# A linear-attention kernel: the level queries of GLA in one product, the level differences in one subtraction

## The chip, the core and the metric

The kernel runs on one core of a Trainium2 chip. The core has a matrix engine (TensorE, PE in the profile; its weight loads are PEld), a vector engine (VectorE, DVE), an activation engine (ScalarE, ACT), a general engine (GpSimd, POOL) and an engine that issues DMAs (SyncE, SP). Each runs its own queue in order and waits on semaphores for the others. The metric is the time of one execution on the device, in microseconds (us).

## The reference, cut to what matters

One step of a two-layer decoder for 512 prompt tokens and 64 sample tokens (8 sequences of 8). Each layer projects the normed input, feeds four recurrent mixers (HGRN2, GLA, RWKV-7, retention), gates and merges them, and ends with a SwiGLU feed-forward. HGRN2 and GLA are gated linear attention: a decay of its own for each key channel and token.

```python
    def step(S, inp):
        qb, kb, vb, gb = inp
        b = jnp.cumsum(gb, axis=2)
        diff = b[:, :, :, None, :] - b[:, :, None, :, :]
        decay = jnp.exp(jnp.where(causal > 0, diff, 0.0)) * causal
        scores = jnp.sum(qb[:, :, :, None, :] * kb[:, :, None, :, :] * decay, axis=-1)
        o = (jnp.einsum('bhts,bhsv->bhtv', scores, vb)
             + jnp.einsum('bhtk,bhkv->bhtv', qb * jnp.exp(b), S))
...
    o_gla, n_gla = gated_linear_attention_chunked(
        _heads(gla_q * GLA_DK ** -0.5, GLA_H), _heads(gla_k, GLA_H),
        _heads(gla_v, GLA_H), _heads(log_a, GLA_H), s_gla)
```

HGRN2 has four heads with 64 key channels each, GLA four with 32; both have 64 value channels a head.

## The kernel before

Channels lie on the 128 partitions and tokens along the free axis. HGRN2 has two tiles of channels with two heads each (nt = 2), GLA one tile with four heads of 32 partitions (nt = 1). `gla_core` (L967) serves both. It takes the running sums B of the log decays and goes over five chunks: four of 128 prompt tokens and one of the 64 sample tokens.

Within a chunk the scores are built by levels: m = 64, 32, 16, 8, 4, 2, 1 for a prompt chunk, m = 4, 2, 1 for the sample chunk. At level m the chunk falls into blocks of 2m tokens; queries of a block's later half (u = 1) meet keys of its earlier half (u = 0), with B at the first token of the later half as the common reference. So the exponents are ref - B for the earlier half and B - ref for the later one, and neither grows. `gla_level` (L1089) does one level:

- L1101 and L1102: two subtractions on VectorE, one per half, into the tile le
- L1103: one exponential on ScalarE over the whole of le, in place
- L1104: the keys times le into lk, on VectorE for HGRN2 and on GpSimd for GLA
- L1111: the queries of the later halves times le into a zero-padded tile that holds every head apart, qt for HGRN2 (two products of 64 partitions) and qg for GLA (four of 32 partitions, and half of the chunk's tokens as columns)

L1018 multiplies the two on TensorE into lvp, with all four heads side by side along the free axis, and `gla_pred` (L1122) copies the valid places of it into the score tile sc on VectorE (L1126). The loop is staggered: the operands of the next level are made ahead of the product of the present one, and the predicated copy of a level comes after that.

The padded tiles come from three-deep rings (`padded`, L1114) that GpSimd zeroes once (L412 to L414); only the diagonal blocks of heads are written afterwards.

The mixers are generators. `mix` (L1612) advances them between the steps of the projection's units, by the paces of PACE (L43): HGRN2 beside the RWKV and GLA projections, GLA beside later projections and gates, RWKV over nearly the whole. The matrix products of the units have weights that are split into two halves of 16 bits (L228 on ScalarE, L229 on VectorE), and their matmuls are L241 to L243. The recurrent RWKV state is updated at L867 on VectorE, after TensorE's product L865, and TensorE's products L815 and L849 wait for it; GpSimd's copy L795 and its other small steps serve the same recurrence. The instructions are put in order on each engine by a planner that works from its own estimates of their costs; the order on an engine is thus not always that of the code.

Of the kernel before, what the change touches and what calls it, by code (L numbers as in the profile page):

```python
# [10 lines left out]
F32 = mybir.dt.float32  # L11
F16 = mybir.dt.float16
I32 = mybir.dt.int32
AF = mybir.ActivationFunctionType
ALU = mybir.AluOpType
PSUM = bass.MemoryType.PSUM
ADD, SUB, MUL, MAX, MIN = ALU.add, ALU.subtract, ALU.mult, ALU.max, ALU.min
# [157 lines left out]
class Net:  # L175
# [159 lines left out]
    def setup(self):  # L335

        nc, t, cp = self.nc, self.io, self.cp
        rows = self.wp.tile([128, GW], F32, tag="raw", name="prow")[:, :128]
        for n, k in PARAMS:
            b = PBASE[n][0]  # L340
# [14 lines left out]
        for i, a in enumerate(self.x0):  # L355
            k, hs = 2 * (i % 4), slice(HW * (i // 4), HW * (i // 4) + HW)
# [16 lines left out]
        for n in ("rw_w0", "rw_a0"):  # L373
            b, k = PBASE[n]
            nc.vector.tensor_scalar(self.pc[:, b:b + 2 * k], self.pc[:, b:b + 2 * k], 0.5, None, op0=MUL)
        b = PBASE["rw_kk"][0]
        nc.vector.tensor_scalar(self.pc[:, b:b + 4], self.pc[:, b:b + 4], 2.0 ** 15, None, op0=MUL)
        b = PBASE["rw_ka"][0]
# [3 lines left out]
        b = PBASE["hg_lb_logits"][0]  # L382
# [15 lines left out]

        self.qt = [cp.tile([128, 4, 64], F32, name=f"qt{i}") for i in range(3)]
        self.qg = [cp.tile([128, 4, 64], F32, name=f"qg{i}") for i in range(3)]  # L400
        self.sc = [cp.tile([128, 4, 128], F32, name=f"sc{i}") for i in range(2)]
        self.scs = cp.tile([64, 4, 64], F32, name="scs")
        self.vz = [cp.tile([128, 2, 256], F32, name=f"vz{i}") for i in range(2)]
# [5 lines left out]
        self.xb = cp.tile([128, 2, 64], F32, name="rw_xb")  # L409
        self.qb = [cp.tile([128, 2, 128], F32, name=f"rt_qb{i}") for i in range(2)]  # L410
        self.nkv = 0
        for a in [*self.kvb, *self.abk, self.ab, self.ub, *self.bb, self.xb, *self.qb, *self.qt, *self.qg,  # L412
                  *self.sc, self.scs, *self.vz]:
            nc.gpsimd.memset(a, 0.0)  # L414
        self.nq = self.nqg = self.nsc = self.nvz = 0
# [551 lines left out]
    def gla_core(self, l, q, k, v, lg, nt, load, result):  # L967
# [3 lines left out]
        nc = self.nc  # L971
        hpt = 4 // nt
        dk = 128 // hpt
        B = lg
# [21 lines left out]
        for c in range(5):  # L996
            samp = c == 4
            n = 64 if samp else 128
            ts = slice(128 * c, 128 * c + n)
# [4 lines left out]
                sc = self.sc[self.nsc % 2]  # L1004
                self.nsc += 1
            lv = [(li, m) for li, m in enumerate(LEVELS) if 2 * m <= (8 if samp else 128)]
            ops = [self.gla_level(q, k, B, nt, ts, n, m) for li, m in lv[:1]]
            prev = None
            for i, (li, m) in enumerate(lv):
                if i + 1 < len(lv):  # L1010
                    ops.append(self.gla_level(q, k, B, nt, ts, n, lv[i + 1][1]))
                if prev is not None:
                    self.gla_pred(*prev)
                yield
                kt, qt = ops[i]
                ps = self.psum("g", [128, 4, 64], f"lvp{nt}")
                for j in range(nt):
                    nc.tensor.matmul(ps[:n, hpt * j:hpt * j + hpt, :n // 2], kt[:, j],  # L1018
                                     qt[:, hpt * j:hpt * j + hpt, :n // 2], start=True, stop=True)
                prev = sc, ps, li, m, n  # L1020
# [4 lines left out]
            w = 8 if samp else 128  # L1025
            nc.scalar.activation(QH, B[:, :, ts], AF.Exp)
            bb = B[:, :, ts].rearrange("p j (c s) -> p j c s", s=w)
# [4 lines left out]
            if samp:  # L1032
                qz = self.padded(nt)
                for h in range(hpt):
                    r = slice(dk * h, dk * h + dk)
# [9 lines left out]
            ops = self.psum("g", [128, 2, 128], "gop")  # L1045
# [40 lines left out]
        result += [O, S]  # L1086
        yield

    def gla_level(self, q, k, B, nt, ts, n, m):  # L1089

        nc = self.nc
        hpt = 4 // nt
        dk = 128 // hpt
        nb = n // (2 * m)
        E = self.t("gt", [128, nt, n], f"le{nt}")
        kt = self.t("gt", [128, nt, n], f"lk{nt}")

        eng = nc.vector
        bb, ee = (a.rearrange("p j (b u i) -> p j b u i", u=2, i=m) for a in (B[:, :, ts], E))
        ref = bb[:, :, :, 1, 0:1].to_broadcast([128, nt, nb, m])  # L1100
        eng.tensor_tensor(ee[:, :, :, 0], ref, bb[:, :, :, 0], op=SUB)  # L1101
        eng.tensor_tensor(ee[:, :, :, 1], bb[:, :, :, 1], ref, op=SUB)  # L1102
        nc.scalar.activation(E, E, AF.Exp)  # L1103
        (nc.vector if nt == 2 else nc.gpsimd).tensor_tensor(kt, k[:, :, ts], E, op=MUL)  # L1104
        qt = self.padded(nt)
        for h in range(hpt):
            r = slice(dk * h, dk * h + dk)
            qq = q[r, :, ts].rearrange("p j (b u i) -> p j b u i", u=2, i=m)[:, :, :, 1]
            ee = E[r].rearrange("p j (b u i) -> p j b u i", u=2, i=m)[:, :, :, 1]
            qo = qt[r, h::hpt, :n // 2].rearrange("p j (b i) -> p j b i", i=m)  # L1110
            nc.vector.tensor_tensor(qo, qq, ee, op=MUL)  # L1111
        return kt, qt

    def padded(self, nt):  # L1114
# [497 lines left out]
    def mix(self, l, prepared):  # L1612
# [3 lines left out]
        for half in range(2):  # L1616
            for i in range(3):
                for _ in range(2):
                    next(units[i])
                if half == 0 and i == 0:  # L1620
                    if l:
                        self.norm_half("attn_norm_w", l, 1)
                    else:
                        self.first_norm(1)
                        setup = self.setup()
                        next(setup)
                if l == 0 and half == 1 and i == 0:
                    run(setup)
# [314 lines left out]
```

## Time and profile before

| what | us |
|---|---|
| median of 3 runs (lowest, highest) | 2242.47 (2237.26, 2242.92) |
| the profiled execution | 2235.82 |
| its span, first to last instruction | 2234.1 |
| PE busy | 2047.3 (92%) |
| PEld busy | 1616.7 (72%) |
| DVE busy | 1677.4 (75%) |
| ACT busy | 1070.6 (48%) |
| POOL busy | 652.0 (29%) |

Busy time is the union of an engine's records. Matmuls are pipelined and their ends are modelled, so a busy TensorE is not yet one at its peak. The chain of work that ended last is followed back from the last instruction, at each step to what released it or to the instruction ahead of it on its engine. A group's row gives its busy time, the mean duration of one instruction, and the idle time of the engine just before, with who ended it. Layer 0 takes the first half of the span, layer 1 the second.

### The profile page before, as it was taken

How to read it: one execution, taken by the hardware profiler on the slowest of the kernel's cores; microseconds unless marked ns; L12 is line 12 of the kernel's file. 1: busy time of each engine (PE TensorE's matmuls, PEld its weight loads, DVE VectorE, ACT ScalarE, POOL GpSimd, SP SyncE). 2: the span in 40 equal slices, each digit the busy share in tenths (PEclk: the TensorE clock that was granted, in tenths of full speed). 3: DMA queues.
4: the chain of work that ended last, by engine and by line, in shares of the span. 5: the costliest groups of instructions: out<-in, count | busy, mean ns of one | idle time of the engine just before them, and what ended most of it. 6: DMA issues, size and time to landing. Idle time of an engine off the chain costs nothing.

```text
span 2234.1 us, 42266 instructions
## 1 busy us (share of the span) xinstructions
PE 2047.3 (92%) x15754; PEld 1616.7 (72%) x15754; DVE 1677.4 (75%) x3719; ACT 1070.6 (48%) x2400; POOL 652.0 (29%) x850
## 2 busy tenths in 40 slices
PE   7988899898989999999998889889998988999998
PEld 5766676686767677777776667768776766777776
DVE  7889856868786899973488996686687768998531
ACT  6554545436454655442466344363554455554332
POOL 2212212245550544320011131222365415443000
PEclk9999999999999999999999999999999999999999
DMA  6312213333436244343421222142344443443431
GB/s 179 82 36 66 54 52 91 94 77 84 108 100 200 59 118 126 88 132 108 120 69 51 54 56 60 51 116 72 79 98 104 124 144 93 118 116 93 126 105 50
DMA packets 373497, 209.58 MB, mean 94 GB/s; under 512 B 59810, under 2 KB 360410, under 8 KB 373292
## 3 DMA queue, kind: packets, MB, share of 16 engines
q1 hardware_dynamic: 365516, 192.73, 31.1%
q0 software_dynamic: 7776, 14.16, 3.5%
q8 instruction: 124, 2.03, 0.4%
q14 instruction: 81, 0.66, 0.1%
HBM read 173.72 MB, written 16.59 MB: 85 GB/s over the span
## 4 chain that ended last, share of the span: by engine, by line
PE 47%; DVE 31%; ACT 8%; issue 7%; DMA 4%; POOL 3%; SPq 0%; DVEq 0%; ACTq 0%; POOLq 0%
PE pb L243 4%; PE pb L241 4%; PE pb L242 4%; PE xb L243 4%; PE xb L242 4%; PE xb L241 4%; DVE hA L1693 3%; DVE hS L1693 2%; DVE whl L229 2%; DVE sc L1734 2%; DVE fy L1765 2%; DVE qg L1111 2%; PE fsS L1720 2%; PE fsS L1718 2%; PE fsS L1719 2%
## 5 line engine op out<-in xcount | busy, mean ns | idle before, releaser
L241 PE MATMUL pb<-h,whl 128*128 128x288 f16 (+1 forms) x1504 | 439.9, 293 | 3.7 <-ACT h L463 2.2
L243 PE MATMUL pb<-h,whl 128*128 128x288 f16 (+1 forms) x1504 | 439.7, 293 | 2.7 <-DVE whl L229 2.7
L242 PE MATMUL pb<-h,whl 128*128 128x288 f16 (+1 forms) x1504 | 439.5, 292 | 0.6 <-DVE h L464 0.4
L229 DVE SCALAR_TENSOR_TENSOR whl<-raw,whl 128x512 f16<-128x512 f32 (+1 forms) x352 | 251.7, 725 | 132.0 <-ACT whl L228 130.3
L243 PEld LDWEIGHTS <-whl 128*128 128x128 f16 (+1 forms) x2784 | 277.3, 100 | 88.4 <-issue 11.0
L242 PEld LDWEIGHTS <-whl 128*128 128x128 f16 (+1 forms) x2784 | 276.7, 99 | 87.4 <-issue 11.0
L241 PEld LDWEIGHTS <-whl 128*128 128x128 f16 (+1 forms) x2784 | 279.0, 100 | 77.0 <-issue 3.6
L228 ACT ACTIVATE whl<-raw 128x512 f16<-128x512 f32 (+1 forms) x352 | 213.0, 616 | 167.4 <-PE pb L243 58.1
L243 PE MATMUL xb<-fa,whl 128*128 128x288 f16 x704 | 201.3, 286 | 0.0
L242 PE MATMUL xb<-fa,whl 128*128 128x288 f16 x704 | 201.3, 286 | 0.0
L241 PE MATMUL xb<-fa,whl 128*128 128x288 f16 x704 | 201.3, 286 | 0.0
L1718 PE MATMUL fsA<-h,hA 128*128 128x288 f16 x432 | 123.5, 286 | 14.4 <-DVE gu L1539 9.1
L1718 PE MATMUL fsS<-st,hS 128*128 128x288 f16 x456 | 131.1, 287 | 6.0 <-ACT hS L1692 6.0
L1720 PE MATMUL fsS<-st,hS 128*128 128x288 f16 x456 | 131.2, 288 | 0.9 <-DVE hS L1693 0.9
L1719 PE MATMUL fsS<-st,hS 128*128 128x288 f16 x456 | 131.1, 287 | 0.0
L1720 PE MATMUL fsA<-h,hA 128*128 128x288 f16 x432 | 123.6, 286 | 1.6 <-DVE hA L1693 1.6
L1719 PE MATMUL fsA<-h,hA 128*128 128x288 f16 x432 | 123.5, 286 | 0.0
L1696 POOL TENSOR_TENSOR raw<-raw 128x512 f32<-128x512 f32 x52 | 79.5, 1529 | 133.8 <-DVE hA L1693 129.7
L1718 PEld LDWEIGHTS <-hS 128*128 128x128 f16 x864 | 85.1, 99 | 35.5 <-ACT hS L1692 14.1
L1693 DVE SCALAR_TENSOR_TENSOR hA<-sraw,hA 128x512 f16<-128x512 f32 x110 | 101.5, 930 | 10.4 <-ACT hA L1692 9.7
L1696 POOL TENSOR_TENSOR sraw<-sraw 128x512 f32<-128x512 f32 x60 | 89.9, 1501 | 50.0 <-DVE hA L1693 45.5
L1720 PEld LDWEIGHTS <-hS 128*128 128x128 f16 x864 | 85.2, 99 | 24.6 <-DVE hS L1693 3.0
(487 smaller groups left out, 5271.1 us busy)
## 6 DMA issues: line engine op xcount, KB each, us to landing
raw<-in_w_in SPq DMA_DIRECT2D x208, 256.0 KB
sraw<-in_w_ffn_in SPq DMA_DIRECT2D x40, 512.0 KB
raw<-in_w_ffn_out SPq DMA_DIRECT2D x80, 256.0 KB
raw<-in_w_ffn_in SPq DMA_DIRECT2D x78, 256.0 KB
x<-xd SPq DMA_DIRECT2D x32, 288.0 KB
raw<-sraw POOLq DMA_DIRECT2D x34, 256.0 KB, 3.3
sraw<-in_w_in SPq DMA_DIRECT2D x32, 256.0 KB
raw<-in_w_out SPq DMA_DIRECT2D x32, 256.0 KB
```

What stands on the lines that cost most here:

```text
L228: nc.scalar.activation(hl[:, 0, :n], raw[:, :n], AF.Copy, scale=WS)
L229: nc.vector.scalar_tensor_tensor(hl[:, 1, :n], raw[:, :n], WS, hl[:, 0, :n], op0=MUL, op1=SUB)
L241: nc.tensor.matmul(ps, wh, hi, start=i == 0, stop=False)
L242: nc.tensor.matmul(ps, wh, lo, start=False, stop=False)
L243: nc.tensor.matmul(ps, wl, hi, start=False, stop=i == len(ks) - 1)
L1111: nc.vector.tensor_tensor(qo, qq, ee, op=MUL)
L1693: nc.vector.scalar_tensor_tensor(hl[:, 1], a, WS, hl[:, 0], op0=MUL, op1=SUB)
L1696: nc.gpsimd.tensor_tensor(dst, a, b, op=op)
L1718: nc.tensor.matmul(ps, w[a][:, 0, k], hi, start=k == 0, stop=False)
L1719: nc.tensor.matmul(ps, w[a][:, 0, k], lo, start=False, stop=False)
L1720: nc.tensor.matmul(ps, w[a][:, 1, k], hi, start=False, stop=k == 3)
L1734: nc.vector.tensor_tensor(o, a, p, op=ADD)
```

## The change

In `gla_level` the two subtractions become one over both halves, B - ref, and the exponential becomes two, one per half, with a scale of -1 for the earlier half and +1 for the later one. This holds for HGRN2 and GLA. For GLA, `gla_core` first lays the queries of the chunk out per head: four copies on GpSimd put head h's 32 partitions into block h of a tile qm of [128, 4, tokens] whose other places are zero. The query operand of a level is then a single product on VectorE over 128 partitions and four blocks, with le broadcast over the blocks. qm has two tiles, used in turn by the chunks, and these are zeroed at the start instead of the three of qg.

```diff
-        for a in [*self.kvb, *self.abk, self.ab, self.ub, *self.bb, self.xb, *self.qb, *self.qt, *self.qg,
+        for a in [*self.kvb, *self.abk, self.ab, self.ub, *self.bb, self.xb, *self.qb, *self.qt, *self.qm,
                   *self.sc, self.scs, *self.vz]:
             nc.gpsimd.memset(a, 0.0)
...
+            qm = None
+            if nt == 1:
+
+                qm = self.qm[c % 2][:, :, :n]
+                for h in range(4):
+                    r = slice(32 * h, 32 * h + 32)
+                    nc.gpsimd.tensor_copy(qm[r, h], q[r, 0, ts])
...
-        eng = nc.vector
-        bb, ee = (a.rearrange("p j (b u i) -> p j b u i", u=2, i=m) for a in (B[:, :, ts], E))
-        ref = bb[:, :, :, 1, 0:1].to_broadcast([128, nt, nb, m])
-        eng.tensor_tensor(ee[:, :, :, 0], ref, bb[:, :, :, 0], op=SUB)
-        eng.tensor_tensor(ee[:, :, :, 1], bb[:, :, :, 1], ref, op=SUB)
-        nc.scalar.activation(E, E, AF.Exp)
+        bb, ee = (a.rearrange("p j (b w) -> p j b w", w=2 * m) for a in (B[:, :, ts], E))
+        nc.vector.tensor_tensor(ee, bb, bb[:, :, :, m:m + 1].to_broadcast([128, nt, nb, 2 * m]), op=SUB)
+        for u, sign in ((0, -1.0), (1, 1.0)):
+            e = ee[:, :, :, m * u:m * u + m]
+            nc.scalar.activation(e, e, AF.Exp, scale=sign)
         (nc.vector if nt == 2 else nc.gpsimd).tensor_tensor(kt, k[:, :, ts], E, op=MUL)
         qt = self.padded(nt)
+        if nt == 1:
+            qq = qm.rearrange("p h (b u i) -> p h b u i", u=2, i=m)[:, :, :, 1]
+            nc.vector.tensor_tensor(qt[:, :, :n // 2].rearrange("p h (b i) -> p h b i", i=m), qq,
+                                    ee[:, :, :, m:].to_broadcast([128, 4, nb, m]), op=MUL)
+            return kt, qt
         for h in range(hpt):
             r = slice(dk * h, dk * h + dk)
             qq = q[r, :, ts].rearrange("p j (b u i) -> p j b u i", u=2, i=m)[:, :, :, 1]
-            ee = E[r].rearrange("p j (b u i) -> p j b u i", u=2, i=m)[:, :, :, 1]
             qo = qt[r, h::hpt, :n // 2].rearrange("p j (b i) -> p j b i", i=m)
-            nc.vector.tensor_tensor(qo, qq, ee, op=MUL)
+            nc.vector.tensor_tensor(qo, qq, ee[r, :, :, m:], op=MUL)
         return kt, qt
```

## Rows read from the trace of the kernel before

**Rows 1.** Busy us (and instructions) of each engine by stretch; then granted clock, DMA share, GB/s

```profile
56.00:180.00 124.00, 112.33 (x854) 89.39 (x852) 108.89 (x308) 61.67 (x137) 23.09 (x47) 0.97 0.24 61
180.00:370.00 190.00, 170.68 (x1257) 136.19 (x1256) 138.90 (x442) 81.38 (x230) 43.25 (x100) 0.96 0.23 58
1160.00:1262.00 102.00, 92.26 (x683) 72.86 (x682) 87.09 (x231) 51.24 (x112) 17.13 (x41) 0.95 0.22 55
1262.00:1460.00 198.00, 179.11 (x1326) 143.18 (x1325) 149.47 (x483) 83.68 (x237) 45.03 (x104) 0.97 0.24 59
```

**Rows 2.** Chain that ended last, by line, in 180:370, 1262:1460 and 56:180

```profile
by line: DVE qg L1111 11.4%; PE pb L243 7.3%; PE pb L241 7.3%; PE pb L242 7.2%; issue 5.1%; PE lvp L1018 3.1%; PE gop L1048 3.0%; ACT le L1103 2.4%; DVE whl L229 2.4%; DVE le L1101 2.2%; DVE le L1102 2.2%; DVE sc L1126 2.1%; PE xvp L815 1.7
by line: DVE qg L1111 12.0%; PE pb L241 6.9%; PE pb L243 6.9%; PE pb L242 6.7%; issue 4.2%; DVE whl L229 3.8%; DVE sc L1126 3.5%; PE lvp L1018 2.7%; PE gop L1048 2.4%; DVE le L1102 2.3%; DVE le L1101 2.3%; ACT le L1103 2.2%; PE xvp L815 1.5
by line: issue 16.8%; PE pb L243 9.3%; PE pb L242 8.8%; PE pb L241 8.7%; DVE whl L229 6.0%; PE lvp L1018 5.4%; DVE qt L1111 4.5%; DVE sc L1126 3.8%; DVE lk L1104 2.5%; DVE rw_wp L920 2.2%; DVE le L1101 2.0%; DVE rw_pr L918 1.9%; DVE le L110
```

**Rows 3.** Groups in 180:370: xcount | busy us, mean ns | idle before, releasers

```profile
L1111 DVE TENSOR_TENSOR qg<-gl_q,le 32x64 f32<-32x64 f32 x112 | 30.1, 269 | 4.5 <-ACT le L1103 3.2
L1111 DVE TENSOR_TENSOR qg<-gl_q,le 32x32 f32<-32x32 f32 x12 | 4.9, 408 | 0.4 <-ACT le L1103 0.3
L1101 DVE TENSOR_TENSOR le<-gl_lg 128x64 f32<-128x64 f32 x28 | 6.4, 229 | 0.3
L1102 DVE TENSOR_TENSOR le<-gl_lg 128x64 f32<-128x64 f32 x28 | 7.0, 250 | 0.0
L1103 ACT ACTIVATE le<-le 128x128 f32<-128x128 f32 x31 | 9.5, 308 | 26.6 <-DVE le L1102 26.6
L1103 ACT ACTIVATE le<-le 128x64 f32<-128x64 f32 x3 | 0.8, 256 | 3.8 <-DVE le L1102 3.8
L1104 POOL TENSOR_TENSOR lk<-gl_k,le 128x128 f32<-128x128 f32 x28 | 15.7, 559 | 80.2 <-ACT le L1103 64.7 <-PE nps L865 10.1 <-PE pb L243 3.0
```

**Rows 4.** Timeline of VectorE (start, us): differences, then an instruction of 128x256

```profile
180.15 0.21 DVE L1101 TENSOR_TENSOR le<-gl_lg 128x64 f32<-128x64 f32 x1
180.28 0.21 DVE L1102 TENSOR_TENSOR le<-gl_lg 128x64 f32<-128x64 f32 x1
...
185.30 0.44 DVE L1126 COPY_PREDICATED sc<-lev,lvp 128x256 f32<-128x256 int32 x1
185.63 0.68 DVE L229 SCALAR_TENSOR_TENSOR whl<-raw,whl 128x512 f16<-128x512 f32 x1
```

**Rows 5.** Groups in 56:180, HGRN2's level loop

```profile
L1104 DVE TENSOR_TENSOR lk<-hg_k,le 128x256 f32<-128x256 f32 x28 | 11.8, 421 | 4.5 <-ACT le L1103 4.5
L1103 ACT ACTIVATE le<-le 128x256 f32<-128x256 f32 x28 | 11.6, 416 | 25.0 <-DVE le L1102 23.2 <-DVE rw_pr L918 1.7
L1101 DVE TENSOR_TENSOR le<-hg_f 128x128 f32<-128x128 f32 x28 | 8.1, 289 | 0.4
```

**Rows 6.** Timeline, GpSimd and VectorE at 226.7 us

```profile
226.69 0.89 POOL L1104 TENSOR_TENSOR lk<-gl_k,le 128x128 f32<-128x128 f32 x1 [4.08 <-ACT le L1103]
...
227.19 0.47 DVE L1111 TENSOR_TENSOR qg<-gl_q,le 32x64 f32<-32x64 f32 x1
```

**Rows 7.** Timeline of ScalarE at 180.6 us

```profile
180.63 0.63 ACT L228 ACTIVATE whl<-raw 128x512 f16<-128x512 f32 x1 [2.90 <-PE pb L243]
181.16 0.29 ACT L1103 ACTIVATE le<-le 128x128 f32<-128x128 f32 x1
```

**Rows 8.** Line L1379: count, duration ns min/median/max, first and last start

```profile
L1379 POOL COPY rt_qb<-rt_q x40: 231/290/1216, 372.9 to 1547.9; 64x128 f32<-64x128 f32 x32, 64x64 f32<-64x64 f32 x8
```

**Rows 9.** TensorE's waits in 180:370: us in total, times, longest

```profile
PE xvp L815 <- DVE rws L867: 7.4, 3, 3.5
```

**Rows 10.** Timeline of VectorE at 255.3 us

```profile
255.35 0.21 DVE L1101 TENSOR_TENSOR le<-gl_lg 128x64 f32<-128x64 f32 x1
255.55 0.48 DVE L1066 SCALAR_TENSOR_TENSOR gs<-gs,glb 128x256 f32<-128x256 f32 x1
```

**Rows 11.** GpSimd's waits in 180:370

```profile
POOL rw_bb L795 <- PE xps L849: 11.2, 4, 8.8
```

More of the change, by code (lines that the diff above doesn't have):

```diff
@@ L400, in setup @@
         self.qg = [cp.tile([128, 4, 64], F32, name=f"qg{i}") for i in range(3)]
+        self.qm = [cp.tile([128, 4, 128], F32, name=f"qm{i}") for i in range(2)]
         self.sc = [cp.tile([128, 4, 128], F32, name=f"sc{i}") for i in range(2)]
@@ L1006, in gla_core @@
             lv = [(li, m) for li, m in enumerate(LEVELS) if 2 * m <= (8 if samp else 128)]
-            ops = [self.gla_level(q, k, B, nt, ts, n, m) for li, m in lv[:1]]
+            qm = None
[4 more added lines that the diff above has]
+                    nc.gpsimd.tensor_copy(qm[r, h], q[r, 0, ts])
+            ops = [self.gla_level(q, qm, k, B, nt, ts, n, m) for li, m in lv[:1]]
             prev = None
@@ L1010, in gla_core @@
                 if i + 1 < len(lv):
-                    ops.append(self.gla_level(q, k, B, nt, ts, n, lv[i + 1][1]))
+                    ops.append(self.gla_level(q, qm, k, B, nt, ts, n, lv[i + 1][1]))
                 if prev is not None:
@@ L1087, in gla_core, with gla_level @@
         yield
-    def gla_level(self, q, k, B, nt, ts, n, m):
+    def gla_level(self, q, qm, k, B, nt, ts, n, m):
         nc = self.nc
```

## The prediction

> **What bounds the kernel now.** I first read the busy time by stretch, to see where the changed lines run and which engine is full there. The level loop of HGRN2 runs from 56 to 180 us in layer 0 and from 1160 to 1262 in layer 1, that of GLA from 180 to 370 and from 1262 to 1460 [rows 1]. In these stretches VectorE is busy for 109 of 124 and 139 of 190 us, TensorE for 112 and 171. Neither is full: TensorE's records leave 11.7 + 19.3 us idle in layer 0, 9.7 + 18.9 in layer 1, 60 us in all. Next comes the chain of work that ended last, to see whose time counts while neither engine is full. In the GLA stretches the largest item of that chain is the very line that is changed: the products qg at L1111 hold 11.4% of 190 us and 12.0% of 198 us, 21.7 + 23.8 = 45.5 us [rows 2]. No single matmul line comes near. So GLA's stretch is a chain that runs through VectorE, with TensorE waiting in pieces behind it.
>
> **The products of GLA's queries.** A level multiplies four heads apart, 32 partitions each. In one layer 112 products of 64 columns take 30.1 us and 12 of 32 columns 4.9 us [rows 3], 35.0 us; four make a set, so 28 + 3 sets become 31 products over 128 partitions. The price of one such product is not in the trace; the nearest rows are a VectorE instruction of 128x256, after which the next starts 0.33 us later [rows 4], and HGRN2's key product of 128x256 with a duration of 421 ns [rows 5]. For the three sample levels (128 columns) I take 289 ns [rows 5]. Low end: 28 x 0.33 + 3 x 0.29 = 10.1 us per layer. The high end comes from GpSimd: at 226.69 GpSimd begins the key product lk and VectorE's head product at 227.19 takes 0.47 us, ending 0.08 us after lk does [rows 6], where an instruction with the same 64 columns takes 0.21 [rows 4]. So it can be held 0.26 us, and a long product 0.42 + 0.26 = 0.68. High end: 28 x 0.68 + 2.4 (half of the 4.9, for the sample levels) = 21.4 us. The mean of the present head products, 269 ns, is 59 above 0.21, and 4 x 59 = 0.24 us a set: today about one hold falls on every set. A single product is held only where lk starts ahead of it; both wait for the same exponential and no row says who is first on the whole, so I count half and take (0.33 + 0.68) / 2 = 0.50, with 1.6 for the sample levels: 15.6 us. VectorE saves 19.4 us per layer (13.6 to 24.9).
>
> Of the 70 us that the products take in both layers 45.5 lie on the chain, 0.65. The chain loses 2 x 19.4 x 0.65 = 25.2 us (17.7 to 32.4).
>
> A rule that speaks against this: the Trainium skill's page "SBUF — State Buffer", section "Who interferes with whom", has VectorE and GpSimd share a read interface when a VectorE instruction has two SBUF inputs, and whichever comes first holds it for its whole length. The hold in [rows 6] agrees with it. By that rule the long product would also push lk back by its own length whenever it is first; it is the second rival below, with its time from rows.
>
> **The differences.** Two subtractions of half the width become one. GLA: means of 229 and 250 ns [rows 3] become one of 289, 0.19 less; but the two overlap, the second starting 0.13 us behind the first [rows 4], and by starts the gain is only 2 x 0.13 - (0.29 - 0.08) = 0.05. HGRN2: 2 x 289 against 421 is 0.16, or 0.08 with that overlap of 0.08 taken off once [rows 5]. I take 0.10 for each of 62 + 62 levels, near the starts, since instructions stand close. On the chain lie 4.4% of 190 + 4.6% of 198 = 17.5 of 26.8 us in GLA, 0.65, and in HGRN2 2.0% of 124 = 2.5 of 8.1 us, 0.31 [rows 2, 3, 5]. That is 6.2 x 0.65 + 6.2 x 0.31 = 6.0 us off the chain (3 to 10).
>
> **The exponentials.** Each level has two in place of one, on ScalarE. GLA: 2 x 256 (64 columns, as in today's sample levels) against 308 ns is 0.20 more; HGRN2: 2 x 308 against 416, also 0.20 [rows 3, 5]. ScalarE starts an instruction 0.10 us before the one ahead has ended [rows 7], which would leave 0.10. I take 0.12, as both are ready at once. ScalarE is busy 81 of 190 us [rows 1], so the 15 us in all find room, but the level waits for the later half: on the chain lie 2.4% of 190 + 2.2% of 198 = 9 of 19 us in GLA, 0.47 [rows 2, 3]; in HGRN2 the line is below the 2.0% that the row still shows, so 0.2 at most. 62 x 0.12 x (0.47 + 0.2) = 5.0 us onto the chain (4 to 8). No row shows an in-place exponential with gaps between its runs, as the small levels will have; were a half as dear as the whole it would be the upper end.
>
> **The copies on GpSimd.** Four copies of 32 partitions a chunk, 40 in all; the nearest row is that of RetNet's copies, 0.23 us at the least and 0.29 in the median for 64 partitions [rows 8], so some 1.0 us a chunk and 10 us together. They are hidden: before its key products GpSimd sits idle for 80.2 us in one GLA stretch, 64.7 of it until ScalarE's exponential [rows 3]. They need only q, which is there since the projection, and a tile last read two chunks earlier. Uncovered they would cost 10 us. But the first level of each chunk now has VectorE wait for GpSimd; queued behind that wait are the weights' second halves (L229) and the RWKV state (L867), for which TensorE waits. That is the third rival. The zeroing at the start touches other tiles once, long before their first use; nothing.
>
> **The sum.** -25.2 - 6.0 + 5.0 = -26 us on the chain; by the bounds -38 to -13. What is late next is TensorE: 26 of its 60 idle us would have to vanish, and some of that idle belongs to other waits, such as those of GLA's chunk ends on ScalarE. I keep 0.7 of it: **-18 us** (-27 to -9). The profiled execution took 2235.82 us, 1.7 more than its span; it is 6.6 below the median of 2242.47, so the same -18 gives 2217.8 for a profiled execution and 2242.5 - 18 = 2224 for a median, which is what I forecast, own range 2215 to 2233.
>
> **Rivals.**
> 1. *The chain is no price list.* Only TensorE's waits that name the delayed RWKV state would go: 7.4 us in layer 0 [rows 9], taken for both, of which the share 19.4 / 35.0 gives 2 x 4.1 = 8 us, less 5 for the exponentials: 2239, no change that can be told. For it: the idle time of TensorE is in small pieces. Against it: the weight of the line on the chain. The same holds if a product with a broadcast operand runs no faster than four.
> 2. *The shared read interface takes it back.* Every product is held or holds lk: VectorE saves 13.6 per layer, the chain -17.7 - 3 + 8 = -13, kept at 0.7: -9, 2233. For it: [rows 6]. Against it: today's sets already pay about one hold each, as worked out above.
> 3. *GpSimd becomes the gate (slower).* The planner places instructions by its own estimates, not as written: a subtraction of the next chunk stands ahead of the state update written before it [rows 10]. If it puts the copies behind one of GpSimd's waits on TensorE, 11.2 us in 4 waits, 2.8 each [rows 11], VectorE stalls with them: 10 chunks x 2.8 = 28 us, less the 18: 2252. It decides from 1.8 us a chunk. Against it: the 64.7 us of idle time in front of lk.
> 4. *A better order.* The chain's whole upper bound goes, -38, and TensorE's other waits keep 5 of it: -33, some 2210. For it: the 60 us of TensorE's idle time [rows 1]. Against it: no other rival would then have cost anything.
>
> **How the numbers follow.** Forecast 0.47, rival 1 0.17, rival 2 0.14, rival 3 0.11, rival 4 0.11. A measurement of this kernel tells 0.3%, 6.7 us, from no change. Faster: 0.47 + 0.14 + 0.11 and a little of rival 1, 0.74; same 0.15; slower 0.11. The range takes in rivals 1, 2 and most of 4 and leaves out rival 3: 2206 to 2243.
>
> **What would show it.** In the changed profile the 62 products should have 128x256 in 0.42 to 0.7 us and some 16 us per layer; VectorE's busy time should fall by 40 to 60 us, ScalarE's rise by some 15 to 25; L1111's qg should leave the top of the chain in GLA's stretches, which together should be 12 to 20 us shorter while HGRN2's stay within 3 us. The forecast is wrong if the stretches keep their length with VectorE emptier (rival 1), if lk grows well past 559 ns (rival 2), or if VectorE shows idle time ended by the GpSimd copies (rival 3).

## The result and the profile after

The median went from 2241.55 us (2237.26 to 2242.92, 4 runs) to 2203.99 (2201.5 to 2207.72, 4 runs): a ratio of 0.9837 with a 95% interval of 0.9817 to 0.9857, 36.5 us by the ratio. Two further comparisons of the same pair gave 0.9844 (0.9827 to 0.9861) and 0.9843 (0.9822 to 0.9864). The forecast was 2224, the range ended at 2206: right in sign, but half the size.

The profiled executions, 2235.82 and 2207.72 us, differ by 28 only. The one of before was on the short side: a second one, of 2245.1 us, has the same lengths up to 520 us to within 0.6 and longer feed-forward stages, which the change does not touch, by 9 us in all. Medians are therefore compared with medians, and stretches with stretches.

The page of after, busy time by engine (us, share of the span, instructions):

```profile
PE 2039.1 (92%) x15754; PEld 1612.3 (73%) x15754; DVE 1636.6 (74%) x3409; ACT 1081.3 (49%) x2524; POOL 682.3 (31%) x889
```

VectorE has 40.8 us and 310 instructions less, ScalarE 10.7 us more, GpSimd 30.3 more. TensorE, with the same 15754 matmuls, has 8.2 us less.

Busy time by stretch, the same four stretches as in [rows 1], cut at the same matmuls to the whole microsecond (window, length, busy us with counts of PE, PEld, DVE, ACT, POOL; granted clock, DMA share, GB/s):

```profile
55.00:179.00 124.00, 112.95 (x846) 89.27 (x847) 107.49 (x281) 63.66 (x164) 26.95 (x55) 0.96 0.24 61
...
179.00:351.00 172.00, 165.13 (x1255) 133.43 (x1253) 119.76 (x311) 83.90 (x264) 54.59 (x112) 0.99 0.25 64
1145.00:1247.00 102.00, 92.63 (x686) 73.37 (x684) 87.43 (x213) 53.45 (x134) 21.74 (x49) 0.95 0.23 57
1247.00:1428.00 181.00, 172.16 (x1326) 139.44 (x1325) 129.52 (x353) 85.95 (x273) 56.00 (x116) 1.00 0.25 63
```

This is the view to learn from. HGRN2's two stretches have their old lengths, 124 and 102 us. GLA's are 18 and 17 us shorter: 388 became 353, nearly the whole gain. Of these 35 us, 22.5 are TensorE's idle time (190 - 170.68 + 198 - 179.11 = 38.2 before, 172 - 165.13 + 181 - 172.16 = 15.7 after). The other 12.5 are TensorE's *busy* time (349.8 to 337.3) for the same work, 2583 and 2581 matmuls. The column after POOL shows what changed beside it: the granted clock rose from 0.96 and 0.97 to 0.99 and 1.00. How far that accounts for the 12.5 us is worked out below the table of the experiments.

The chain that ended last, in GLA's stretch of layer 0 (179 to 352 us), as in [rows 2]:

```profile
by line: PE pb L242 12.4%; PE pb L243 12.4%; PE pb L241 12.4%; PE lvp L1026 6.2%; PE gop L1056 3.5%; issue 3.4%; DVE le L1107 2.2%; DVE qg L1115 2.2%; ACT le L1110 1.8%; PE ub L241 1.8%; PE ub L242 1.7%; PE ub L243 1.7%; DMA raw<-in_w_in 1.
```

The products fell from 11.4% to 2.2%; the projection's matmuls took their place. The groups of this stretch, beside [rows 3]:

```profile
L1115 DVE TENSOR_TENSOR qg<-qm,le 128x256 f32<-128x256 f32 x28 | 12.7, 453 | 3.6 <-ACT le L1110 3.5
L1107 DVE TENSOR_TENSOR le<-gl_lg 128x128 f32<-128x128 f32 x28 | 10.7, 386 | 0.1
L1115 DVE TENSOR_TENSOR qg<-qm,le 128x128 f32<-128x128 f32 x3 | 1.5, 492 | 0.5 <-ACT le L1110 0.4
...
L1110 ACT ACTIVATE le<-le 128x64 f32<-128x64 f32 x62 | 12.6, 250 | 13.1 <-DVE le L1107 11.8 <-POOL rw_r L574 0.5 <-PE ops L872 0.4
...
L1111 POOL TENSOR_TENSOR lk<-gl_k,le 128x128 f32<-128x128 f32 x28 | 19.9, 711 | 65.4 <-ACT le L1110 43.7 <-PE pb L243 6.4 <-DVE scs L1137 4.6
L1014 POOL COPY qm<-gl_q 32x128 f32<-32x128 f32 x8 | 2.9, 365 | 0.7 <-DVE qg L1115 0.3
```

A level's product takes 453 ns where the set of four took 4 x 269. GpSimd's key product grew from 559 to 711.

### The profile page after: what moved, and what is told of

The parts are those of the page before. It is cut to its first block, busy times and chain, and to the rows that moved or that the text cites. A ratio compares the mean times of both kernels' runs of the same rounds, so it can differ in the third digit from the quotient of the medians.

```text
span 2205.9 us, 42236 instructions
## 1 busy us (share of the span) xinstructions
PE 2039.1 (92%) x15754; PEld 1612.3 (73%) x15754; DVE 1636.6 (74%) x3409; ACT 1081.3 (49%) x2524; POOL 682.3 (31%) x889
## 4 chain that ended last, share of the span: by engine, by line
PE 47%; DVE 28%; ACT 8%; issue 7%; DMA 5%; POOL 3%; SPq 1%; DVEq 0%; ACTq 0%; POOLq 0%
PE pb L243 5%; PE pb L242 5%; PE pb L241 5%; PE xb L243 4%; PE xb L242 4%; PE xb L241 4%; DVE hA L1704 4%; DVE hS L1704 3%; DVE sc L1745 2%; DVE fy L1776 2%; DVE whl L229 2%; DVE su L1745 2%; PE fsS L1731 2%; PE fsS L1729 2%; PE fsS L1730 2%
## 5 line engine op out<-in xcount | busy, mean ns | idle before, releaser
L242 PEld LDWEIGHTS <-whl 128*128 128x128 f16 (+1 forms) x2784 | 275.4, 99 | 88.0 <-issue 13.5
L243 PEld LDWEIGHTS <-whl 128*128 128x128 f16 (+1 forms) x2784 | 275.1, 99 | 88.0 <-issue 12.7
L1729 PEld LDWEIGHTS <-hS 128*128 128x128 f16 x864 | 85.7, 99 | 35.9 <-ACT hS L1703 13.7
## 6 DMA issues: line engine op xcount, KB each, us to landing
raw<-in_w_in SPq DMA_DIRECT2D x208, 256.0 KB
raw<-in_w_ffn_out SPq DMA_DIRECT2D x80, 256.0 KB
raw<-in_w_ffn_in SPq DMA_DIRECT2D x78, 256.0 KB
raw<-sraw POOLq DMA_DIRECT2D x34, 256.0 KB, 3.3
sraw<-in_w_in SPq DMA_DIRECT2D x32, 256.0 KB
raw<-in_w_out SPq DMA_DIRECT2D x32, 256.0 KB
```

Source lines behind the costliest of these rows:

```text
L242: nc.tensor.matmul(ps, wh, lo, start=False, stop=False)
L243: nc.tensor.matmul(ps, wl, hi, start=False, stop=i == len(ks) - 1)
L1729: nc.tensor.matmul(ps, w[a][:, 0, k], hi, start=k == 0, stop=False)
```

## Where a microsecond of VectorE went: one place in two kernels

Layer 0's GLA stretch holds a place that shows the mechanism. VectorE in the kernel before, from 303.9 us (start, us, instruction), with the RWKV state update rws at L867:

```profile
303.86 1.08 DVE L1111 TENSOR_TENSOR qg<-gl_q,le 32x64 f32<-32x64 f32 x4 [0.38 <-ACT le L1103]
...
306.08 1.08 DVE L1111 TENSOR_TENSOR qg<-gl_q,le 32x64 f32<-32x64 f32 x4 [0.44 <-ACT le L1103]
307.17 0.23 DVE L1101 TENSOR_TENSOR le<-gl_lg 128x64 f32<-128x64 f32 x1
307.31 0.22 DVE L1102 TENSOR_TENSOR le<-gl_lg 128x64 f32<-128x64 f32 x1
307.44 0.34 DVE L867 SCALAR_TENSOR_TENSOR rws<-nps,reb,rsd 128x128 f32<-128x128 f32 x1
```

TensorE there, and behind it the busy time from 300 to 320 us and of three pieces of 5 us:

```profile
303.76 0.28 PE L865 MATMUL nps<-ryn,rtk 128*128 128x128 f32 x1
...
304.51 0.29 PE L243 MATMUL pb<-h,whl 128*128 128x288 f16 x1
307.84 0.80 PE L815 MATMUL xvp<-rtk,abk 128*128 128x128 f32 x2 [3.05 <-DVE rws L867]
...
309.18 0.45 PE L241 MATMUL pb<-h,whl 128*128 128x288 f16 x1
309.42 0.45 PE L242 MATMUL pb<-h,whl 128*128 128x288 f16 x1
```

```profile
300.00:320.00 20.00, 16.95 (x112) 13.53 (x111) 14.18 (x53) 7.83 (x26) 4.68 (x11) 0.83 0.18 48
...
305.00:310.00 5.00, 2.16 (x10) 1.89 (x11) 3.56 (x14) 1.88 (x6) 1.33 (x3) 0.68 0.06 9
310.00:315.00 5.00, 5.00 (x27) 3.77 (x26) 2.40 (x10) 1.24 (x3) 1.96 (x6) 0.63 0.15 43
...
345.00:350.00 5.00, 4.86 (x21) 3.60 (x22) 0.60 (x4) 1.11 (x4) 1.80 (x6) 0.50 0.03 7
```

The state's input nps was there at 304.04 (303.76 + 0.28), but two query sets and their differences stood ahead of the update on VectorE. TensorE waited 3.05 us for it, and afterwards its matmuls start 0.24 us apart (309.18, 309.42), at the lower of the clock's two levels, 1.2 GHz: the granted clock was 1.00 up to 305 us, then 0.68 and 0.63. The same place after the change, on VectorE, on TensorE, and by stretch from 290 us:

```profile
296.09 0.43 DVE L1115 TENSOR_TENSOR qg<-qm,le 128x256 f32<-128x256 f32 x1
296.44 0.55 DVE L1107 TENSOR_TENSOR le<-gl_lg 128x128 f32<-128x128 f32 x1
296.90 0.34 DVE L868 SCALAR_TENSOR_TENSOR rws<-nps,reb,rsd 128x128 f32<-128x128 f32 x1
```

```profile
297.13 0.29 PE L243 MATMUL pb<-h,whl 128*128 128x288 f16 x1
297.30 0.49 PE L816 MATMUL xvp<-rtk,abk 128*128 128x128 f32 x2
```

```profile
290.00:310.00 20.00, 20.00 (x162) 16.65 (x160) 13.33 (x41) 9.59 (x36) 6.96 (x15) 1.00 0.21 54
```

No wait, a clock of 1.00, and 162 matmuls in 20 us where there were 112. In the whole stretch of 173 us TensorE's wait for rws fell from 7.4 us [rows 9] to 0.9. The wait of 3.05 us so cost twice: once while TensorE stood, and once more in the slower matmuls behind it. The longest wait for rws, 3.5 us [rows 9], did the same: it ended at 345.1 us, and the clock from 345 to 350 us was 0.50. The Trainium skill's page "TensorE: Matmul & The Clock Gate", Part 1, tells of a clock that drops to half when TensorE has stood idle; the rows of this place agree, with 3.05 us of idle time and starts of 0.24 against 0.12 us.

Not every wait is followed by the lower clock. In the same profile TensorE waited 2.62 us for hsq (L514, up to 229.1 us), and the clock stayed at 1.00:

```profile
225.00:230.00 5.00, 2.38 (x14) 1.40 (x13) 3.27 (x10) 4.94 (x8) 0.89 (x1) 1.00 0.23 52
230.00:235.00 5.00, 5.00 (x42) 4.20 (x40) 3.81 (x9) 3.03 (x6) 0.77 (x1) 1.00 0.22 56
```

In a second profile of the same kernel the same wait (2.60 us) was followed by a clock of 0.80 and 0.86 in these two pieces. The changed kernel has this wait too (2.64 us), and behind it the only piece of lower clock in its two GLA stretches, 0.66 from 225 to 230 us. So the second cost of a wait is not the same from one execution to the next.

## The experiments

All ratios are to the kernel before on the same chip, with 95% intervals. "GLA" means both GLA stretches, cut at the same matmuls as above; "idle" is their length less TensorE's busy time; both are good to about 1 us. A diff is against the changed kernel, for e7 and e9 against the kernel before and for e13 against e12.

| kernel | ratio | GLA us | VectorE busy | TensorE busy | idle |
|---|---|---|---|---|---|
| before | 1 | 388 | 288.4 | 349.8 | 38.2 |
| after | 0.9837 | 353 | 249.3 | 337.3 | 15.7 |
| e1 product only | 0.9875 | 358 | 256.0 | 339.1 | 18.9 |
| e2 difference only | 0.9964 | 380 | 282.0 | 346.8 | 33.2 |
| e3 product twice | 0.9870 | 360 | 266.6 | 337.9 | 22.1 |
| e4 four of 128 | 0.9893 | 359 | 261.3 | 338.8 | 20.2 |
| e9 before, five products | 1.0007 | 387 | 298.5 | 344.3 | 42.7 |
| e12 before, four of 128 | 0.9907 | 363 | 268.2 | 340.8 | 22.2 |
| e13 before, five of 128 | 0.9917 | 366 | 278.7 | 341.7 | 24.3 |
| e14 e5 and e8 together | 0.9833 | 354 | 249.4 | 340.3 | 13.7 |

What TensorE's busy time differs by goes with the clock. A stretch of length L with a mean granted clock c has lost (1 - c) x L against a clock of 1.00: 0.04 x 190 + 0.03 x 198 = 13.5 us before, 0.01 x 172 = 1.7 after. Busy time less this loss is 336.3 and 335.6 us, and it lies between 335 and 338 in all ten kernels. This is an estimate: the clock has two decimals, which leaves some 2 us open, and no kernel changed the clock alone.

### The parts apart: e1, e2, e7

e1 has the layout tile and the single product, with the old differences and exponential:

```diff
...
-        nc.vector.tensor_tensor(ee, bb, bb[:, :, :, m:m + 1].to_broadcast([128, nt, nb, 2 * m]), op=SUB)
-        for u, sign in ((0, -1.0), (1, 1.0)):
-            e = ee[:, :, :, m * u:m * u + m]
-            nc.scalar.activation(e, e, AF.Exp, scale=sign)
+        ref = bb[:, :, :, 1, 0:1].to_broadcast([128, nt, nb, m])
+        nc.vector.tensor_tensor(ee[:, :, :, 0], ref, bb[:, :, :, 0], op=SUB)
+        nc.vector.tensor_tensor(ee[:, :, :, 1], bb[:, :, :, 1], ref, op=SUB)
+        nc.scalar.activation(E, E, AF.Exp)
...
```

> The copies and the single product of GLA as in the change; the two subtractions and the one exponential of before are kept. Theory (VectorE's time for the four head products is what GLA's stretches wait for): nearly the whole gain, ratio to the kernel before 0.984 to 0.988, the two GLA stretches together some 25 us shorter or more. Rival (the single difference and the split exponentials bring a third of the gain or more): 0.989 to 0.992.

Measured: 2212.41 us, 0.9875 (0.9862 to 0.9889), 28 us less than before, as the theory had it. e2 has the new difference and the two exponentials, with the four head products and no copies:

```diff
...
-            if nt == 1:
+            if False:
                 qm = self.qm[c % 2][:, :, :n]
...
-        if nt == 1:
+        if False:
...
```

> One subtraction and two exponentials as in the change; four head products from the queries and no copies, as before. Theory: VectorE gains some 0.05 to 0.10 us a level and ScalarE pays 0.10, so 0.997 to 1.000. Rival (they bring a third or more): 0.990 to 0.994. A third possibility, that the planner's new order by itself is worth something, would show as a gain with VectorE's set of four unchanged at 1.1 us.

Measured: 2232.74 us, 0.9964 (0.9951 to 0.9976), 8.1 us less, between the two expectations. The two GLA stretches are 8 us shorter. The same matmuls start 2.0 us earlier at the head of GLA's stretch of layer 0, little more than executions of one kernel differ by there (177.3 to 178.7 us in the changed kernel). VectorE saves 6.4 us in the GLA stretches; its instructions are in another order as well, and no kernel has the single difference in the old order, so what the order gave is open. The two parts add up: 28.0 + 8.1 = 36.1 of 36.5 us. e7 is the kernel before with its exponential in two halves:

```diff
-        nc.scalar.activation(E, E, AF.Exp)
+        for u in range(2):
+            nc.scalar.activation(ee[:, :, :, u], ee[:, :, :, u], AF.Exp)
```

> The kernel before with the exponential of each level in two halves (HGRN2 and GLA), the two subtractions kept: 124 more ScalarE instructions, 0.10 to 0.20 us each. As forecast (the level waits for the later half): 3 to 6 us slower, 1.0013 to 1.0027. Rival (hidden, since ScalarE is half idle and a level is made one step ahead of its product): 0.9995 to 1.0005, and the whole of the difference's gain then belongs to the subtraction.

Measured: 1.0008 (0.9998 to 1.0018): 1.8 us, from -0.4 to 4.0. The second half comes to nothing, or to little, in the whole. The interval reaches from no change into the forecast 3 to 6 us, so the two expectations are not parted; the order of instructions is another here too, from 89 us on. ScalarE's groups show the halves, in GLA's stretch of layer 0, at 251 ns each:

```profile
L1104 ACT ACTIVATE le<-le 128x64 f32<-128x64 f32 x62 | 13.2, 251 | 21.0 <-DVE le L1101 18.5 <-DVE le L1102 2.2
```

### Is it VectorE's time? e4 against e2, e12 against before

e4 is the changed kernel with four products of 128 partitions and 64 columns in place of the one:

```diff
-            nc.vector.tensor_tensor(qt[:, :, :n // 2].rearrange("p h (b i) -> p h b i", i=m), qq,
-                                    ee[:, :, :, m:].to_broadcast([128, 4, nb, m]), op=MUL)
+            for h in range(4):
+                nc.vector.tensor_tensor(qt[:, h:h + 1, :n // 2].rearrange("p h (b i) -> p h b i", i=m), qq[:, h:h + 1],
+                                        ee[:, :, :, m:], op=MUL)
```

> The changed kernel with four products of 128 partitions and 64 columns, one per head's block, in place of one of 256 columns: as many instructions as before, but all start at the same partition. Theory (the four were dear because each starts at another partition and waits for the end of the one ahead of it): starts 0.14 us apart, a set in 0.6 us or with one hold 0.85, so about half of the gain, 0.988 to 0.993. Rival (the number of instructions is what costs): a set of 1.1 us as before and no gain, 0.997 to 1.002.

Measured: 2215.76 us, 0.9893 (0.9878 to 0.9908). Number, width and mean duration of the products are those of before (272 against 268 ns), and yet two thirds of the gain is there. The timelines show the difference: a set of four that starts at four partitions takes 1.08 us (306.08 above), one that starts at partition 0 throughout takes 0.87, since each product begins before the last has ended:

```profile
186.38 0.87 DVE L1116 TENSOR_TENSOR qg<-qm,le 128x64 f32<-128x64 f32 x4
```

The group row of e12, a kernel that comes below and has the same products, shows it for a whole stretch: 112 products of 276 ns hold 24.5 us, where 112 of 269 ns held 30.1 [rows 3].

```profile
L1117 DVE TENSOR_TENSOR qg<-qm,le 128x64 f32<-128x64 f32 x112 | 24.5, 276 | 3.5 <-ACT le L1110 3.4
```

The Trainium skill's page "VectorE: DVE Perf Modes", "Two Vector instructions with no wait between them", has such an instruction held until the ones ahead have finished when its operands start in another group of 32 partitions than theirs; the rows agree.

It happens that e4 and e2 issue the same instructions in the same order on VectorE, ScalarE and TensorE; only the partitions differ, and GpSimd's copies, which are work added. VectorE's busy time in the GLA stretches differs by 20.7 us and the medians by 17.0. So 17 us came from the time that the products occupy VectorE, with the order kept.

e9 spoke against that: it is the kernel before with the first head's product issued twice a level.

```diff
-            nc.vector.tensor_tensor(qo, qq, ee, op=MUL)
+            for _ in range(2 if nt == 1 and h == 0 else 1):
+                nc.vector.tensor_tensor(qo, qq, ee, op=MUL)
```

> The kernel before with the first head's product of each GLA level issued twice: 62 VectorE instructions more, 0.27 us each between starts, 17 us. Theory (with VectorE as the bound of GLA's stretches its time counts whole): 15 to 19 us slower, 1.0065 to 1.0085. Rival (the share of the products on the chain, 0.65, times the 0.7 that the forecast kept): 8 us, 1.003 to 1.004.

Measured: 2239.91 us, 1.0007 (0.9995 to 1.0019). Both expectations missed, the theory by at least 10 us: VectorE is busy 10.1 us longer in the GLA stretches and nothing was lost. But here the planner had 62 instructions more to place, and VectorE's order is another from 181 us on. Hence two kernels that separate order and time. e12 is the kernel before with e4's products and copies (e1's and e4's edits together), and has before's order on VectorE, ScalarE and TensorE; e13 has e9's five products with 128 partitions, and e9's order:

```diff
-            for h in range(4):
+            for h in (0, 0, 1, 2, 3):
                 nc.vector.tensor_tensor(qt[:, h:h + 1, :n // 2].rearrange("p h (b i) -> p h b i", i=m), qq[:, h:h + 1],
                                         ee[:, :, :, m:], op=MUL)
```

> The kernel before with its two differences and its one exponential; GpSimd lays the queries out per head and VectorE's four products each take 128 partitions and 64 columns (32 in the short chunk), so that all four start at partition 0. Instruction for instruction VectorE, ScalarE and TensorE have the order of the kernel before; only the time that the four products occupy VectorE changes, by the starts of e4 against e2 some 19 us over both layers. Theory A (time that products occupy VectorE in the GLA stretches counts, about 0.87 us for each, as between e2 and e4): 17 us less than before, about 2223 us (2219 to 2228), GLA stretches 7 to 9 us shorter each. Theory B (e1 and e4 gained by the instruction order that followed from another list of instructions, not by VectorE's time): no change against before, 2237 to 2243 us.

> e9 with products of 128 partitions: the list and the order of instructions on VectorE, ScalarE and TensorE are those of e9 (first head's product issued twice), the occupied time that of e12 plus one product a level, some 8 to 12 us. Theory A alone: 7 to 10 us over e12, about 2231 us. Theory C (the planner puts a longer list in an order that takes the added product's time back, which is why e9 showed nothing): within 3 us of e12, about 2223 us, as e9 is within 3 us of the kernel before. Theory B: as e9, 2237 to 2243 us.

Measured: e12 2217.3 us, 0.9907 (0.9884 to 0.993), 21 us less than before; e13 2219.73, 0.9917 (0.9897 to 0.9938). Theory B is out: with the old order kept, 20.2 us less of VectorE's time gave 21. The stretches of e12 and of e9:

```profile
181.00:356.00 175.00, 165.28 (x1255) 133.17 (x1254) 128.89 (x438) 81.50 (x230) 51.12 (x112) 0.99 0.25 63
1250.00:1438.00 188.00, 175.56 (x1325) 141.51 (x1323) 139.32 (x482) 83.12 (x236) 52.73 (x116) 0.98 0.24 62
```

```profile
179.00:366.00 187.00, 166.36 (x1252) 133.09 (x1251) 143.63 (x465) 79.44 (x230) 43.44 (x100) 0.99 0.24 59
1262.00:1462.00 200.00, 177.93 (x1326) 141.94 (x1324) 154.88 (x513) 81.62 (x237) 44.94 (x104) 0.97 0.23 58
```

In e12, 16.0 us of TensorE's idle time went and 9.0 of its busy time, at a clock of 0.99 and 0.98. At the place of the last section its wait for rws is 1.53 us in e12, 3.05 in before. In e9 the added 10.1 us did bring 4.5 us of idle time (38.2 to 42.7), but TensorE's busy time fell by 5.5: layer 0 ran at 0.99 where before had 0.96. And between e12 and e13, 10.5 us of VectorE's time brought 2.1 us of idle time and 2.4 of the whole, hardly more than the noise of this difference (some 2.3 us). So time that the same list saves counted nearly whole (e12 21 for 20.2, e4 against e2 17 for 20.7), and of an instruction added to the list little showed in the whole: nothing in e9, about a fifth of its time in e13. That the planner's new order takes the rest is likely, not shown: no kernel had five products in the order of four. Why the clock fell less in e9 is open too.

### What bounds the changed kernel: e3, e5, e6, e8, e14

e3 issues the single product twice.

```diff
-            nc.vector.tensor_tensor(qt[:, :, :n // 2].rearrange("p h (b i) -> p h b i", i=m), qq,
-                                    ee[:, :, :, m:].to_broadcast([128, 4, nb, m]), op=MUL)
+            for _ in range(2):
+                nc.vector.tensor_tensor(qt[:, :, :n // 2].rearrange("p h (b i) -> p h b i", i=m), qq,
+                                        ee[:, :, :, m:].to_broadcast([128, 4, nb, m]), op=MUL)
```

> The changed kernel with each single product of GLA issued twice into the same tile (the second repeats the first), 62 more VectorE instructions of 0.42 us, some 24 us. Theory (VectorE's time counts until TensorE is full, and TensorE is nearly full now): a third to a half of it comes back, 8 to 12 us over the changed kernel, ratio 0.987 to 0.990. Rival (the order that the planner found is the gain, not VectorE's time): as the changed kernel, 0.983 to 0.985. Rival (VectorE is still the bound): all 24 us, 0.994 or more.

Measured: 2211.3 us, 0.987 (0.9856 to 0.9883), 7 over the changed kernel, for 17.3 us more of VectorE's busy time in the GLA stretches. That is a little under the theory's 8 to 12 us and above the 0.983 to 0.985 of the rival by which the order alone is the gain. The order is not kept here either, so 7 us is no price of VectorE's time alone. e5 has GLA's key products on VectorE:

```diff
-        (nc.vector if nt == 2 else nc.gpsimd).tensor_tensor(kt, k[:, :, ts], E, op=MUL)
+        nc.vector.tensor_tensor(kt, k[:, :, ts], E, op=MUL)
```

> The changed kernel with GLA's key product lk on VectorE in place of GpSimd: GpSimd no longer reads beside the single product, VectorE gets 62 instructions more, 0.20 us each between starts, 12 us. Theory (TensorE is nearly full in GLA's stretches, so VectorE's time counts at about the 0.28 that issuing the product twice showed): 3 to 4 us over the changed kernel, 0.985 to 0.988. Rival (the holds between lk and the product still cost the level loop time): at or below the changed kernel, 0.980 to 0.983.

Measured: 2201.88 us, 0.9826 (0.9814 to 0.9839), level with the changed kernel. The groups of GLA's stretch in layer 0 show what GpSimd's key product beside them costs VectorE's instructions:

```profile
L1115 DVE TENSOR_TENSOR qg<-qm,le 128x256 f32<-128x256 f32 x28 | 11.7, 417 | 0.0
L1111 DVE TENSOR_TENSOR lk<-gl_k,le 128x128 f32<-128x128 f32 x28 | 8.4, 299 | 6.2 <-ACT le L1110 5.8 <-issue 0.2
L1107 DVE TENSOR_TENSOR le<-gl_lg 128x128 f32<-128x128 f32 x27 | 7.6, 282 | 0.1
```

Without a key product beside it on GpSimd, the product takes 417 ns instead of 453 and the difference 282 instead of 386. This pays for about half of the 8.4 us that the key products add (12.7 - 11.7 and 10.7 - 7.6 us, 4.1 together).

e6 makes the layout copies in the first two chunks of a layer only; the levels of the other three chunks then read the queries of an earlier chunk.

```diff
-                for h in range(4):
+                for h in range(4 if c < 2 else 0):
```

> The changed kernel without GpSimd's copies in three of a layer's five GLA chunks (their queries are those of an earlier chunk): 24 of 40 copies gone. Theory (copies hidden in GpSimd's idle time): as the changed kernel, 0.983 to 0.985. Rival (VectorE waits for them at each chunk's first level): 24 x 0.4 us gained, 0.979 to 0.981.

Measured: 2205.85 us, 0.984 (0.9823 to 0.9858): the 24 copies left out, of 40, cost nothing that shows. None of VectorE's waits in the changed kernel's GLA stretch of layer 0 ends with a copy. e8 lays HGRN2's queries out per head as well, with a tile qn and one product for each of the two channel tiles; qm and qn are one tile each, in place of two of qm:

```diff
...
-            if nt == 1:
-                qm = self.qm[c % 2][:, :, :n]
-                for h in range(4):
-                    r = slice(32 * h, 32 * h + 32)
-                    nc.gpsimd.tensor_copy(qm[r, h], q[r, 0, ts])
+            qm = (self.qm if nt == 1 else self.qn)[c % 2][:, :, :n]
+            for h in range(hpt):
+                r = slice(dk * h, dk * h + dk)
+                nc.gpsimd.tensor_copy(qm[r, h::hpt], q[r, :, ts])
...
```

> The changed kernel with HGRN2's queries laid out per head once a chunk as well, so that its two products of 64 partitions become two of 128 partitions that start at the same partition; the layout tiles of GLA and HGRN2 are one each in place of two of GLA. VectorE: a set from 0.58 us to 0.41, 10 us in all, in HGRN2's stretches. Theory (VectorE's time counts nearly whole where TensorE is not full): 4 to 10 us under the changed kernel, 0.979 to 0.982. Rival (HGRN2's stretches wait for TensorE and for chains through other lines, as they were not shortened by the single difference): as the changed kernel, 0.983 to 0.986.

Measured: 2201.81 us, 0.9832 (0.9816 to 0.9848), level with the changed kernel. e14 takes e5 and e8 together, beside the changed kernel once more (e15):

> The changed kernel with e5 and e8 together: GLA's key products on VectorE, so that nothing of GpSimd holds the query product, and HGRN2's queries laid out per head too. If the rest of the gain is bounded by TensorE, whose records leave 7 and 9 us idle in the changed kernel's GLA stretches: 2199 to 2204 us, within 5 us of the changed kernel. If VectorE still sets the end of these stretches, the key products (62, some 0.25 us each by starts) cost 8 to 15 us: 2212 to 2220.

> The changed kernel beside e14, on the same chip: 2204 to 2207 us.

Measured: e14 2201.07 us, 0.9833 (0.9813 to 0.9853), e15 2203.68, 0.9843 (0.9822 to 0.9864). The stretches of e14:

```profile
177.00:349.00 172.00, 165.11 (x1254) 133.55 (x1253) 119.48 (x341) 83.67 (x264) 35.72 (x85) 0.99 0.26 65
1242.00:1424.00 182.00, 175.15 (x1328) 141.74 (x1327) 129.89 (x386) 85.89 (x273) 38.38 (x91) 0.98 0.25 62
```

Idle time of 13.7 us is left in 354. None of e5, e8 and e14 beats the changed kernel by more than the intervals, which speaks for TensorE as what now sets GLA's stretch. Oddly for the second theory that e14 was to tell apart, VectorE's busy time did not rise (249.4 against 249.3), since its instructions are shorter, as in e5: the product takes 416 ns and the difference 283. So e14 did not load VectorE as meant, and the reading rests on TensorE's idle time and on e3.

### The same kernels again: e10, e11

> The kernel before once more, for a second profile. If the first profile was an execution with short feed-forward stages (all five other traces have them 2 to 5 us longer per layer), this one has the marks of the others there and a time near the median of 2240. If the changes themselves lengthen the feed-forward, it has the marks of the first profile.

> The changed kernel once more, beside the same runs of the kernel before as the fifth product: 0.982 to 0.986, and GLA's stretches within 1 us of those of the first profile.

Measured: before 2245.1 us in one execution, after 2206.18, 0.9844 (0.9827 to 0.9861). GLA's stretches of the second profile of before are 190 and 200 us, of after 172 and 181.

## Why the prediction was right or wrong

**What bounds the kernel.** Right: the GLA stretches were a chain through VectorE with TensorE waiting behind it, HGRN2's were not. Nearly all of the gain is in the former. HGRN2's stretches kept their lengths within 1 us, as forecast (under 3). The 1.9 us given to its differences is less than executions of one kernel differ by there (223 to 227 us for both stretches of the changed kernel), so no run shows it.

**The products.** The cost was right: 25.3 + 3.0 us in both layers against 2 x 15.6 forecast, so these lines save 20.8 us a layer where I had 19.4. Two things were not seen. Part of what the four products cost was that they began at four different partitions and ran one after another, 20 us of VectorE's time in e12. The 0.24 us a set that I read from the mean of 269 ns is not this: e4's products have a mean of 272 ns too, and overlap. And the hold that I counted on the product (0.50 us each, 0.45 measured) fell on the differences behind it: the first of the two takes 329 ns in e1 where it took 229, and the single one 386 in the change where it takes 305 in e2. So VectorE's 40.8 us come from the products: GLA's differences occupy it for 24.4 us in both layers, overlaps counted once, against 24.6 before.

The weight looks right, 25.2 us off the chain against 28 (25 to 31) in e1, but that is partly luck. The forecast kept 0.7 of the 25.2, 17.6 us, and that is close to what TensorE's idle time lost in e1's GLA stretches, 19.3. Another 10.7 us there are TensorE's busy time, of which the weight on the chain knows nothing.

**The differences and the exponentials.** -6.0 and +5.0 were forecast, together -1; e2 measured -8.1 (-11 to -5.4), 5.0 us of it in TensorE's idle time and 3.0 in its busy time in the GLA stretches. So this term was mis-sized, but between its two halves it is not settled. e7 gives the exponentials 1.8 us (-0.4 to 4.0) where I had 5.0 on the chain and, with the 0.7, 3.5 in the whole: less, but not clear of it. I let the later half lie on the chain by the weight that the whole exponential had there. ScalarE's busy time rose by 10.7 us, under the forecast 15 to 25.

**The copies.** Hidden, as said (e6), so rival 3 has no ground. **Rival 2** described something real: the key product did go from 559 to 711 ns, and it holds the differences, but little of that shows in the whole: e5 and e14, which free VectorE of it, stay within 4 us of the changed kernel. **Rival 1** is out: 22.5 us of idle time went in the GLA stretches, not the 8 of the waits that name rws. **Rival 4**, 2210, came nearest, but out of TensorE's idle time alone.

**The sum.** This is the step that failed. It takes the whole gain out of TensorE's idle time: "26 of its 60 idle us would have to vanish", "I keep 0.7 of it", 18 us. In the GLA stretches the idle time gave 22.5 of 38.2. The 0.7, behind which no row stands, was thus not far off, and the 4.5 us more are about what e2's idle time gave beyond the forecast. But 12.5 us more came out of TensorE's *busy* time, for which the sum had no term: the same matmuls ran at a granted clock of 0.99 and 1.00 instead of 0.96 and 0.97. Both numbers of before stood in [rows 1]. By the working below the table, the matmuls there lost 13.5 us to the lower clock and 1.7 after, a difference of 11.8, which agrees with the 12.5 to within the decimals. With exponentials at nothing and no discount the same sum gives -25.2 - 6.0 = -31, 2211; that is nearer, but without the term that was missing.

**What was to show it.** Products of 128x256 in 0.42 to 0.7 us: 0.45. Some 16 us of them a layer: 14.2. VectorE 40 to 60 us less: 40.8. qg off the top of the chain: yes. The GLA stretches 12 to 20 us shorter: 35, the miss.

**What stays open.** Why an added instruction costs so little (e9, e13), what the new order gave in e2, why the clock fell less in e9 than in before, and why it falls behind one wait and not behind another of much the same length. The profiles are one execution each (three of after, two of before), and the clock's share of a gain was not changed by itself in any kernel.

## What to carry to other kernels

Where TensorE's busy time is close to the length of a stretch but its granted clock there is below 1, price a removed wait with the matmuls behind it: read the clock of the stretch first, and put in a term of its own, with (1 - clock) x length as its upper end. Four small VectorE instructions on slices that start at different partitions did not overlap here; the same number on 128 partitions did, and a layout copy on an idle engine bought that. What VectorE saved without another order counted nearly whole; where instructions were added and the planner's order changed, one instruction's time was a poor guide to its price.

## What had not been expected of the hardware

- Four products that start at partitions 0, 32, 64 and 96 take 1.08 us, four over all 128 partitions 0.87, though each has the same duration or a longer one: less work on each instruction was dearer.
- A single wait of 3.05 us of TensorE was followed by matmuls 0.24 us apart in place of 0.12, so that 112 instead of 162 matmuls ran in 20 us. A wait of 2.6 us was followed by the lower clock in one execution of the same kernel and not in another.
- GpSimd's key product holds back differences as well as products: 386 ns with it beside them, 282 without.
